# Down projection of three quarters of the FFN by Strassen's scheme, its products between blocks of the up projection

## The chip, the cores and the metric

The kernel runs on one core of one Trainium2 chip. The metric is the device time of one execution in microseconds (us), the median over several runs. The times and rows below come from the kernel as it was before the change.

## What is computed

One post-norm layer of an encoder, batch 1, 512 tokens, width 1024. The first sublayer mixes tokens (a state-space branch and a dilated attention branch, gated, projected) and ends in a LayerNorm. The change touches the second sublayer only:

```
f = jnp.square(jax.nn.relu(h @ w_up)) @ w_down      # w_up 1024 x 4096, w_down 4096 x 1024
h = layer_norm(alpha * h + f, ln2_g, ln2_b)         # alpha = 2 ** 0.25
```

All data are float32. To keep precision each operand is split into a part rounded to the matmul's type (hi) and the remainder (lo), and a product is three matmuls: hi x hi, hi x lo, lo x hi (`mm3`, lines 134 to 136).

## The kernel before

TensorE multiplies a stationary block of 128 x 128 by up to 512 columns and adds into one of eight banks of PSUM. The 4096 inner units are 32 blocks of 128. Up gives, for one block, 128 units x 512 tokens: 8 steps over the 1024 inputs, 3 matmuls each (`up_mm`, line 914), so 24 matmuls of 512 columns. ScalarE takes the relu out of PSUM (line 960), VectorE squares it (961), ScalarE rounds it to "fh" (962), VectorE forms the remainder "fl" (963).

Down works in two halves f of 16 blocks, each after its 16 up blocks, and in two column halves c of 512 (lines 946 to 999). For a pair of unit blocks and a column half there is one weight tile of 128 x 1024 floats, 512 KB. For each, `down_mm` issues 4 token tiles x 2 blocks x 3 = 24 matmuls. When all pairs are done, VectorE adds the bank into the residual "h1" (993 in the first half, with alpha; 998 in the second, followed by LayerNorm statistics, 999). In the last half and columns the last four pairs (ND) are held back and worked tile by tile, so that the LayerNorm of one token tile (941 to 943, 1001 to 1006) runs under the matmuls of the next.

Weights come through one stream, `ws` (class `Stream`, lines 73 to 126): SyncE's queue (SP) loads a raw tile (three buffers, line 87), ScalarE casts it to "wh" (108), VectorE subtracts to "wl" (109), two buffers each, one tile ahead of use. These two splits have raised priority. The first four up blocks (NU) have their weights split early into the pool "wu" and run in two halves of 256 tokens while the first LayerNorm ends.

The order of instructions on each engine is made by a scheduler at compile time from data dependencies, buffer slots and priorities (the order of the text, where nothing else decides). A pool opened where another was closed waits for the tiles there. GpSimd does nothing in this part of the kernel; earlier it adds and multiplies tiles for the state-space branch (lines 361, 366, 435, 485).

Of the kernel before, what the change touches and what calls it, by code (L numbers as in the profile page):

```python
# [43 lines left out]
def hybrid_layer_kernel(ctx: ExitStack, tc: tile.TileContext, t: dict, out: bass.AP):  # L44
# [817 lines left out]

    rot = [3, 4, 0, 1, 6, 7, 5, 2]
    nrot = [0]

    def next_bank(name):
        nrot[0] += 1
        return bank(rot[(nrot[0] - 1) % 8], name)
# [76 lines left out]
    st2 = [lp.tile([P, 3, 6], F32, name=f"st2_{i}") for i in range(4)]  # L945
    for f in range(2):
        ff = []
        if f == 0:
            g2 = load_ln(1)
        for i in range(16):  # L950
            if f == 0 and i < NU:
                ps = pre[i]
                up_mm(ps, *wu[i], slice(256, 512))
            else:
                ps = next_bank(f"ps_u{f}_{i}")
                up_mm(ps, *ws.get(), slice(0, 512))
            rl = fp.tile([P, S], F32, name=f"rl{f}_{i}", tag="rl", bufs=2)
            fh = fp.tile([P, S], F32R, name=f"fh{f}_{i}", tag="fh", bufs=17)
            fl = fp.tile([P, S], F32R, name=f"fl{f}_{i}", tag="fl", bufs=17)
            act.activation(rl, ps, AF.Relu)  # L960
            dve.tensor_mul(rl, rl, rl)
            act.copy(fh, rl)
            dve.tensor_sub(fl, rl, f32(fh))
            ff.append((fh, fl))
        if f == 0:
            wu_ctx.close()
            held["dn"] = ctx.enter_context(tc.tile_pool(name="dn", bufs=1, side="right", reuse_waits="tile"))
        for c in range(2):
            cs = slice(c * 512, (c + 1) * 512)
            tail = ND if (f, c) == (1, 1) else 0  # L970
            pss = [[next_bank(f"ps_d{f}_{c}_{i}_{q}") for q in range(2 if tail and i == 3 else 1)] for i in range(4)]

            def down_mm(i, kp, w, parts=(0, 1)):
                ts_ = slice(i * P, (i + 1) * P)
                n = 512 // len(pss[i])
                for q in range(len(pss[i])):
                    if q in parts:
                        for kk in range(2):
                            k = kp * 2 + kk
                            ws_ = slice(kk * 512 + q * n, kk * 512 + q * n + n)  # L980
                            mm3(pss[i][q][:, :n], [(ff[k][0][:, ts_], ff[k][1][:, ts_])], [(w[0][:, ws_], w[1][:, ws_])], first=(k == 0), last=(k == 15))

            for kp in range(8 - tail):
                w = ws.get()
                for i in range(4):
                    down_mm(i, kp, w)
            wt = [ws.get() for _ in range(tail)]
            for i in range(4):
                for part in ((0,), (1,)) if len(pss[i]) > 1 else ((0, 1),):
                    for q in range(tail):  # L990
                        down_mm(i, 8 - tail + q, wt[q], part)
                if f == 0:
                    dve.scalar_tensor_tensor(h1[i][:, cs], h1[i][:, cs], ALPHA, pss[i][0], op0=ALU.mult, op1=ALU.add)
                else:
                    n = 512 // len(pss[i])
                    for q, ps in enumerate(pss[i]):
                        hs = slice(c * 512 + q * n, c * 512 + q * n + n)
                        dve.tensor_add(h1[i][:, hs], h1[i][:, hs], ps[:, :n])
                        dve.bn_stats(st2[i][:, c + q, :], h1[i][:, hs])
                if tail:  # L1000
                    mv = lp.tile([P, 32], F32, name=f"mvb{i}", tag="bmv", bufs=2)
                    dve.bn_aggr(mv[:, 0:2], st2[i][:, :2 + i // 3, :])
# [65 lines left out]
```

## Time and profile before

| what | value |
|---|---|
| median of 3 runs | 1027.06 us (1026.61 to 1027.87) |
| the profiled execution | 1027.38 us |
| its span, first to last instruction | 1025.6 us |
| granted TensorE clock, mean | 0.999 of full |
| instructions | 13697 |
| HBM read, written | 128.25 MB, 11.30 MB |

The profile is of one execution. Its span leaves 1.8 us of the device time outside. Engines are PE (TensorE matmul), PEld (its weight load, which overlaps), DVE (VectorE), ACT (ScalarE), POOL (GpSimd) and SP (SyncE, which issues the DMAs). A group is named by line, engine, operation and tiles, output before input; "L109" is line 109. Idle time of an engine is put down to what released it. Matmuls are pipelined, so that the duration of one is longer than the step from one to the next.

### The profile page before, as it was taken

The page shows a single profiled execution, that of the slowest core. Times are in us where ns is not written, and L with a number is a line of the kernel's source. Part 1 is how long each engine was busy: PE and PEld are TensorE (multiplying, and loading weights), DVE is VectorE, ACT ScalarE, POOL GpSimd, SP SyncE. Part 2 cuts the span into 40 slices and gives each one's busy share as a digit, 9 for nine tenths or more (in the row PEclk, how much of TensorE's full clock was granted, in tenths as well). Part 3 has the DMA queues.
Part 4 walks back from the last instruction along what each step waited for, and adds up shares of the span by engine and source line. Part 5 has one row for each costly group of instructions (what it writes and reads, how often), then busy time and mean ns, then how long its engine had stood idle before and what let it go on. Part 6 is the DMA issues. An engine that isn't in the chain of part 4 may idle for free.

```text
span 1025.6 us, 13697 instructions
## 1 busy us (share of the span) xinstructions
PE 1016.2 (99%) x5169; PEld 842.0 (82%) x5169; DVE 651.5 (64%) x1035; ACT 501.5 (49%) x977; POOL 73.8 (7%) x66
## 2 busy tenths in 40 slices
PE   9999999999999999999999999999999999999997
PEld 7888888888888888888778788898888888888886
DVE  4296979689979897975985285844432333443336
ACT  4444877468857875764773353223431223333120
POOL 0000201221121022112000000000000000000000
PEclk9999999999999999999999999999999999999999
DMA  6445355425653564464853278112233333333322
GB/s 237 149 150 144 113 196 166 147 78 173 179 153 111 167 203 140 150 214 154 288 155 104 62 250 289 46 42 75 90 103 101 86 100 103 94 92 103 101 84 82
DMA packets 48449, 140.42 MB, mean 137 GB/s; under 512 B 6528, under 2 KB 7424, under 8 KB 48128
## 3 DMA queue, kind: packets, MB, share of 16 engines
q1 hardware_dynamic: 48240, 139.30, 43.4%
q8 instruction: 40, 0.66, 0.3%
q10 hardware_dynamic: 144, 0.26, 0.1%
q14 instruction: 25, 0.20, 0.1%
HBM read 128.25 MB, written 11.30 MB: 136 GB/s over the span
## 4 chain that ended last, share of the span: by engine, by line
PE 90%; DVE 5%; ACT 2%; DMA 2%; issue 1%; POOL 0%; DVEq 0%; ACTq 0%; POOLq 0%
PE ps_u L135 6%; PE ps_u L136 6%; PE ps_d L136 6%; PE ps_u L134 6%; PE ps_d L134 6%; PE ps_d L135 6%; PE ps_pa L134 3%; PE ps_z L134 3%; PE ps_z L136 3%; PE ps_z L135 3%; PE ps_pa L135 3%; PE ps_pa L136 3%; PE ps_x L134 3%; PE ps_x L136 2%; PE ps_x L135 2%; PE ps_yo L481 2%
## 5 line engine op out<-in xcount | busy, mean ns | idle before, releaser
L109 DVE TENSOR_TENSOR wl<-wraw,wh 128x1024 fp32r<-128x1024 f32 (+1 forms) x165 | 201.4, 1224 | 234.7 <-ACT wh L108 230.2
L108 ACT CAST wh<-wraw 128x1024 fp32r<-128x1024 f32 (+1 forms) x165 | 171.3, 1042 | 260.8 <-PE ps_d L136 108.6
L135 PE MATMUL ps_u<-htl,wh 128*128 128x512 f32 (+1 forms) x288 | 105.3, 366 | 0.3 <-DVE htl L909 0.3
L134 PE MATMUL ps_u<-hth,wh 128*128 128x512 f32 (+1 forms) x288 | 105.3, 366 | 0.0
L136 PE MATMUL ps_u<-hth,wl 128*128 128x512 f32 (+1 forms) x288 | 105.2, 365 | 0.0
L135 PE MATMUL ps_d<-wl,fh 128*128 128x512 f32 (+1 forms) x272 | 102.5, 377 | 0.0
L134 PE MATMUL ps_d<-wh,fh 128*128 128x512 f32 (+1 forms) x272 | 102.4, 377 | 0.0
L136 PE MATMUL ps_d<-wh,fl 128*128 128x512 f32 (+1 forms) x272 | 102.4, 377 | 0.0
L135 PEld LDWEIGHTS ps_u<-htl,wh 128*128 128x128 f32 x288 | 54.3, 189 | 9.2 <-DVE htl L909 0.5
L136 PEld LDWEIGHTS ps_u<-hth,wl 128*128 128x128 f32 x288 | 54.3, 189 | 8.8
L134 PEld LDWEIGHTS ps_u<-hth,wh 128*128 128x128 f32 x288 | 54.2, 189 | 8.9 <-ACT hth L908 0.3
L135 PEld LDWEIGHTS ps_d<-wl,fh 128*128 128x128 f32 x272 | 51.2, 188 | 9.5
L134 PEld LDWEIGHTS ps_d<-wh,fh 128*128 128x128 f32 x272 | 51.2, 188 | 9.4
L136 PEld LDWEIGHTS ps_d<-wh,fl 128*128 128x128 f32 x272 | 51.2, 188 | 9.4
L134 PE MATMUL ps_pa<-yh,wh 128*128 128x512 f32 x128 | 52.1, 407 | 0.0
L450 DVE SCALAR_TENSOR_TENSOR U<-bc,acr,U 128x128 f32<-128x128 f32 x128 | 46.6, 398 | 8.6 <-ACT U L448 8.5
L134 PE MATMUL ps_g<-xh,wh 128*128 128x512 f32 x128 | 51.5, 402 | 0.0
L134 PE MATMUL ps_z<-xh,wh 128*128 128x512 f32 x128 | 50.9, 398 | 0.0
L134 PE MATMUL ps_x<-xh,wh 128*128 128x512 f32 x128 | 50.9, 398 | 0.0
L136 PE MATMUL ps_g<-xh,wl 128*128 128x512 f32 x128 | 50.0, 391 | 0.4 <-DVE wl L109 0.4
L135 PE MATMUL ps_pa<-yl,wh 128*128 128x512 f32 x128 | 50.1, 392 | 0.2 <-DVE yl L561 0.2
L136 PE MATMUL ps_pa<-yh,wl 128*128 128x512 f32 x128 | 50.1, 391 | 0.0
(262 smaller groups left out, 2185.3 us busy)
## 6 DMA issues: line engine op xcount, KB each, us to landing
wraw<-in_w_in_dram SPq DMA_DIRECT2D x68, 512.0 KB, 3.5
bc<-dr_acr SPq DMA_DIRECT2D x32, 512.0 KB, 4.4
wraw<-in_w_up_dram SPq DMA_DIRECT2D x32, 512.0 KB, 3.6
wraw<-in_w_dn_dram SPq DMA_DIRECT2D x32, 512.0 KB, 3.6
be<-dr_ear SPq DMA_DIRECT2D x32, 256.0 KB, 4.5
wraw<-in_w_ps_dram SPq DMA_DIRECT2D x16, 512.0 KB, 3.8
dr_gate<-g SPq DMA_DIRECT2D x16, 256.0 KB, 2.1
wraw<-in_w_out_dram SPq DMA_DIRECT2D x8, 512.0 KB, 4.5
```

Source lines behind the costliest of these rows:

```text
L108: act.copy(h[:, :width], r[:, :width])
L109: dve.tensor_sub(l[:, :width], r[:, :width], f32(h[:, :width]))
L134: pe.matmul(ps, lh, rh, start=(first and i == 0), stop=False)
L135: pe.matmul(ps, lh, rl, start=False, stop=False)
L136: ins = pe.matmul(ps, ll, rh, start=False, stop=(last and i == n - 1))
L450: dve.scalar_tensor_tensor(U[:, ch(c)], bcs[0][:, hh, ch(c)], acr[:, c, h:h + 1], U[:, ch(c)], op0=ALU.subtract, op1=ALU.min)
L481: pe.matmul(po[d][:, ch(c)], prev[d, c][:, pr * P:(pr + 1) * P], C[:, ch(c)], start=True, stop=True)
```

## The change

The 32 unit blocks become four chunks of 8. Chunks 0 to 2 go through a Strassen scheme in Winograd's form: tokens, units and columns are each cut in two, so that activations are 2 x 2 blocks (a11 to a22, each 4 unit blocks x 256 tokens), weights 2 x 2 quarters (b11 to b22, 1 MB each), and 7 block products stand for 8. The sums of blocks are made on GpSimd in place (`prep_product`), the split into hi and lo after the sum. A product is 24 matmuls into two banks (`product`); its results go into h1 at once, on VectorE or GpSimd. Each product of chunk ch stands behind an up block of chunk ch + 1. Chunk 3 is done as before, pair by pair, with the last column half tile by tile. The activations of a chunk stay unsplit in "r" tiles; the tiles of h (hth, htl) now lie in a pool that is closed after up, and the weights that are held back and the second LayerNorm's constants are placed there. `next_bank` goes. The cut diff (in the deleted loop only the stream's part is shown; the rest of it is printed above):

```diff
-NU, ND = 4, 4
+NU = 4
+UP_ORDER = [range(8), [4, 5, 6, 7, 0, 1, 2, 3]]
+DN_ORDER = [6, 7, 4, 5]
...
     h1 = [lp.tile([P, D], F32, name=f"h1_{i}") for i in range(4)]
-    hth = lp.tile([P, KT, S], F32R, name="hth")
-    htl = lp.tile([P, KT, S], F32R, name="htl")
-    lng = []
-
-    def load_ln(i):
-        g = lp.tile([P, 2, D], F32, name=f"ln{i}", tag="ln", bufs=1)
...
-    for f in range(2):
-        for i in range(16):
-            if f or i >= NU:
-                ws.add(t["w_up"][f * 16 + i])
-        for c in range(2):
-            for i in range(8):
-                ws.add(t["w_dn"][f, c, i], hold=("dn", i) if (f, c) == (1, 1) and i >= 8 - ND else None)
+    for ch in range(4):
+        for b in UP_ORDER[ch > 0]:
+            if ch or b >= NU:
+                ws.add(t["w_up"][ch * 8 + b])
+    for c in range(2):
+        for i in DN_ORDER:
+            ws.add(t["w_dn"][1, c, i], hold=("dn", i) if c else None)
...
+    r2 = {}
+    def up_block(ch, b):
+        if b % 4 == 0:
+            r2[ch, b // 4] = fp.tile([P, 4, S], F32, name=f"r{ch}_{b // 4}", tag=f"r{b // 4}", bufs=1 + b // 4)
+        if ch == 0 and b < NU:
+            ps = pre[b]
+            up_mm(ps, *wu[b], slice(256, 512))
+        else:
+            ps = bank((0, 1)[b % 2] if ch == 0 and b < 6 else (6, 7)[b % 2], f"ps_u{ch}_{b}")
+            up_mm(ps, *ws.get(), slice(0, 512))
+        r = r2[ch, b // 4][:, b % 4, :]
+        act.activation(r, ps, AF.Relu)
+        dve.tensor_mul(r, r, r)
+    for b in range(NU):
+        up_block(0, b)
+    wu_ctx.close()
+    wq_ctx = ExitStack()
+    qp = wq_ctx.enter_context(tc.tile_pool(name="qp", bufs=1, side="right", reuse_waits="tile"))
+    quarter = {}
+    def load_quarters(ch):
+        for half, c in ((0, 0), (0, 1), (1, 1), (1, 0)):
+            q = qp.tile([P, 2, 1024], F32, name=f"wq{ch}_{half}{c}", tag="wq", bufs=4)
+            for j in range(2):
+                dma.dma_start(q[:, j, :], t["w_dn"][ch // 2, c, (ch % 2) * 4 + half * 2 + j])
+            quarter[ch, half, c] = q
+    def prep_product(ch, p):
+        b11, b12, b22, b21 = [quarter[ch, *x] for x in ((0, 0), (0, 1), (1, 1), (1, 0))]
+        lo, hi = slice(0, 256), slice(256, 512)
+        a11, a21 = r2[ch, 0][:, :, lo], r2[ch, 0][:, :, hi]
+        a12, a22 = r2[ch, 1][:, :, lo], r2[ch, 1][:, :, hi]
+        a, asum = {1: (a11, None), 5: (a21, (a21, a22, ALU.add)), 6: (a21, (a21, a11, ALU.subtract)), 7: (a11, (a22, a21, ALU.subtract)),
+                   3: (a21, (a12, a21, ALU.subtract)), 2: (a12, None), 4: (a22, None)}[p]
+        w, wsum = {1: (b11, None), 5: (b11, (b12, b11)), 6: (b11, (b22, b11)), 7: (b12, (b22, b12)),
+                   3: (b22, None), 2: (b21, None), 4: (b21, (b21, b11))}[p]
+        if asum:
+            pool.tensor_tensor(a, asum[0], asum[1], op=asum[2])
+        ah = fp.tile([P, 4, 256], F32R, name=f"ah{ch}{p}", tag="ah", bufs=2)
+        al = fp.tile([P, 4, 256], F32R, name=f"al{ch}{p}", tag="al", bufs=2)
+        act.copy(ah, a)
+        dve.tensor_sub(al, a, f32(ah))
+        wc = []
+        for j in range(2):
+            if wsum:
+                pool.tensor_sub(w[:, j, :], wsum[0][:, j, :], wsum[1][:, j, :])
+            h = qp.tile([P, 1024], F32R, name=f"ch{ch}{p}{j}", tag="ch", bufs=2)
+            l = qp.tile([P, 1024], F32R, name=f"cl{ch}{p}{j}", tag="cl", bufs=2)
+            act.copy(h, w[:, j, :])
+            dve.tensor_sub(l, w[:, j, :], f32(h))
+            wc.append((h, l))
+        return ah, al, wc
+    BANKS = [(0, 1), (3, 4), (5, 2)]
+    npr = [0]
+    def product(ch, p, ops):
+        ah, al, wc = ops
+        pss = [bank(n, f"ps_p{ch}{p}_{n}") for n in BANKS[npr[0] % 3]]
+        npr[0] += 1
+        for j in range(2):
+            for q in range(2):
+                ts_ = slice(q * P, (q + 1) * P)
+                for kk in range(2):
+                    ws_ = slice(kk * 512, kk * 512 + 512)
+                    k = 2 * j + kk
+                    mm3(pss[q], [(ah[:, k, ts_], al[:, k, ts_])], [(wc[j][0][:, ws_], wc[j][1][:, ws_])], first=(k == 0), last=(k == 3))
+        def add(rows, c, q, term, scaled=False, eng=dve):
+            h = h1[rows * 2 + q][:, c * 512:(c + 1) * 512]
+            if scaled and ch == 0:
+                dve.scalar_tensor_tensor(h, h, ALPHA, term, op0=ALU.mult, op1=ALU.add)
+            else:
+                eng.tensor_add(h, h, term)
+        for q, ps in enumerate(pss):
+            if p == 1:
+                v[q] = fp.tile([P, S], F32, name=f"v{ch}_{q}", tag="v", bufs=2)
+                act.copy(v[q], ps)
+                add(0, 0, q, v[q], True, pool)
+            elif p == 5:
+                add(1, 1, q, ps, True)
+                add(0, 1, q, ps, True)
+            elif p == 6:
+                dve.tensor_add(v[q], v[q], ps)
+                add(0, 1, q, v[q], eng=pool)
+            elif p == 7:
+                dve.tensor_add(v[q], v[q], ps)
+                add(1, 0, q, v[q], True, pool)
+                add(1, 1, q, v[q], eng=pool)
+            else:
+                add(*{3: (0, 1), 2: (0, 0), 4: (1, 0)}[p], q, ps)
+    v = {}
+    load_quarters(0)
+    for b in range(NU, 8):
+        up_block(0, b)
+    ops = prep_product(0, 1)
+    for ch in range(3):
+        seq = [1, 5, 6, 7, 3, 2, 4]
+        for n, p in enumerate(seq):
+            up_block(ch + 1, UP_ORDER[1][n])
+            product(ch, p, ops)
+            if n < 6:
+                ops = prep_product(ch, seq[n + 1])
+        if ch < 2:
+            load_quarters(ch + 1)
+        up_block(ch + 1, UP_ORDER[1][7])
+        if ch < 2:
+            ops = prep_product(ch + 1, 1)
+    wq_ctx.close()
+    ht_ctx.close()
+    dn = held["dn"] = ctx.enter_context(tc.tile_pool(name="dn", bufs=1, side="right", reuse_waits="tile"))
+    g2 = load_ln(dn, 1)
+    ff = {}
+    def split_pair(n):
+        i = DN_ORDER[n] - 4
+        src = r2[3, i // 2][:, (i % 2) * 2:(i % 2) * 2 + 2, :]
+        if n % 2:
+            fh = fp.tile([P, 2, S], F32R, name=f"fh{n}", tag="ah", bufs=2)
+            fl = fp.tile([P, 2, S], F32R, name=f"fl{n}", tag="al", bufs=2)
+        else:
+            hl = fp.tile([P, 4, S], F32R, name=f"fhl{n}", tag="r1", bufs=2)
+            fh, fl = hl[:, 0:2, :], hl[:, 2:4, :]
+        act.copy(fh, src)
+        dve.tensor_sub(fl, src, f32(fh))
+        ff[n] = (fh, fl)
...
+    def down_mm(ps, i, n, w, q, width):
+        ts_ = slice(i * P, (i + 1) * P)
+        for kk in range(2):
+            ws_ = slice(kk * 512 + q * width, kk * 512 + (q + 1) * width)
+            mm3(ps[:, :width], [(ff[n][0][:, kk, ts_], ff[n][1][:, kk, ts_])], [(w[0][:, ws_], w[1][:, ws_])], first=(n == 0 and kk == 0), last=(n == 3 and kk == 1))
+
+    def add_out(ps, i, col, width, slot):
+        hs = slice(col, col + width)
+        dve.tensor_add(h1[i][:, hs], h1[i][:, hs], ps[:, :width])
+        dve.bn_stats(st2[i][:, slot, :], h1[i][:, hs])
+
+    for n in range(4):
+        split_pair(n)
+    pss = [bank(n, f"ps_d0_{n}") for n in (3, 4, 5, 2)]
+    for n in range(4):
+        w = ws.get()
+        for i in range(4):
+            down_mm(pss[i], i, n, w, 0, 512)
+    wt = [ws.get() for _ in range(4)]
+    for i in range(4):
+        add_out(pss[i], i, 0, 512, 0)
+    for i in range(4):
+        parts = 2 if i == 3 else 1
+        for q in range(parts):
+            ps = bank((0, 1, 6, 7, 3)[i + q], f"ps_d1_{i}{q}")
+            for n in range(4):
+                down_mm(ps, i, n, wt[n], q, 512 // parts)
+            add_out(ps, i, 512 + q * 256, 512 // parts, 1 + q)
...
```

## Rows read from the trace of the kernel before

**Rows 1.** The page of the profiled execution: span, busy time, chain that ended last.
```profile
span 1025.6 us, 13697 instructions
...
PE 1016.2 (99%) x5169; PEld 842.0 (82%) x5169; DVE 651.5 (64%) x1035; ACT 501.5 (49%) x977; POOL 73.8 (7%) x66
...
PE 90%; DVE 5%; ACT 2%; DMA 2%; issue 1%; POOL 0%; DVEq 0%; ACTq 0%; POOLq 0%
```

**Rows 2.** Busy time by stretch: us from:to, length, busy of each engine, clock, DMA share, GB/s.
```profile
691.40:1018.60 327.20, 327.20 (x1490) 272.81 (x1488) 132.50 (x159) 94.26 (x119) 0.00 (x0) 1.00 0.31 93
```

**Rows 3.** VectorE in order of time: start, length, line, operation (up, then down).
```profile
719.74 1.23 DVE L109 TENSOR_TENSOR wl<-wraw,wh 128x1024 fp32r<-128x1024 f32 x1 [2.24 <-ACT wh L108]
725.17 1.23 DVE L109 TENSOR_TENSOR wl<-wraw,wh 128x1024 fp32r<-128x1024 f32 x1 [2.23 <-ACT wh L108]
...
779.76 1.23 DVE L109 TENSOR_TENSOR wl<-wraw,wh 128x1024 fp32r<-128x1024 f32 x1 [4.21 <-ACT wh L108]
785.20 1.23 DVE L109 TENSOR_TENSOR wl<-wraw,wh 128x1024 fp32r<-128x1024 f32 x1 [4.21 <-ACT wh L108]
```

**Rows 4.** Waits from 690 us on: total us, times, longest.
```profile
ACT wh L108 <- PE ps_d L136: 108.6, 26, 4.5
```

**Rows 5.** Groups by line from 600 us on: busy us, mean ns, idle before.
```profile
L109 DVE TENSOR_TENSOR wl<-wraw,wh 128x1024 fp32r<-128x1024 f32 x72 | 87.8, 1225 | 172.7 <-ACT wh L108 172.6
...
L108 ACT CAST wh<-wraw 128x1024 fp32r<-128x1024 f32 x71 | 74.3, 1053 | 186.5 <-PE ps_d L136 108.6 <-PE ps_u L135 53.9 <-DMA wraw<-in_w_up_dram 9.7
...
L963 DVE TENSOR_TENSOR fl<-rl,fh 128x512 fp32r<-128x512 f32 x32 | 22.2, 693 | 22.0 <-ACT fh L962 22.0
...
L993 DVE SCALAR_TENSOR_TENSOR h<-h,ps_d 128x512 f32<-128x512 f32 x8 | 5.3, 685 | 2.5 <-PE ps_d L136 2.5
```

**Rows 6.** Busy time by stretch, where the loads are densest.
```profile
600.00:625.00 25.00, 25.00 (x112) 20.70 (x111) 21.17 (x29) 10.43 (x13) 0.00 (x0) 1.00 0.88 303
```

**Rows 7.** GpSimd's operations by line: ns min/median/max, first and last start.
```profile
L361 POOL TENSOR_TENSOR yt<-yt,be x16: 1268/1291/1847, 151.9 to 474.9; 128x512 f32<-128x512 f32 x16
L435 POOL TENSOR_TENSOR pv<-pv,etot x16: 1045/1055/1960, 102.1 to 414.0; 128x512 f32<-128x512 f32 x16
L485 POOL TENSOR_TENSOR be<-be x16: 732/779/1377, 126.1 to 464.6; 128x256 f32<-128x256 f32 x16
```

**Rows 8.** GpSimd and VectorE in order of time, where they overlap.
```profile
214.95 1.22 DVE L109 TENSOR_TENSOR wl<-wraw,wh 128x1024 fp32r<-128x1024 f32 x1
...
215.11 1.96 POOL L435 TENSOR_TENSOR pv<-pv,etot 128x512 f32<-128x512 f32 x1 [2.53 <-DVE pv L436]
...
216.08 0.74 DVE L284 SCALAR_TENSOR_TENSOR acc<-ps_B,vec,acc 128x510 f32<-128x510 f32 x1
...
109.04 1.05 POOL L435 TENSOR_TENSOR pv<-pv,etot 128x512 f32<-128x512 f32 x1 [2.01 <-DVE pv L436]
...
109.07 1.56 DVE L418 TENSOR_TENSOR xwl<-xw,xwh 128x512 fp32r<-128x512 f32 x1
...
171.92 1.52 POOL L366 TENSOR_TENSOR sq<-sq,sq 128x512 f32<-128x512 f32 x1 [1.47 <-ACT sq L364]
...
172.22 1.77 DVE L286 SCALAR_TENSOR_TENSOR x<-x,acc 128x512 f32<-128x512 f32 x1
```

**Rows 9.** VectorE in order of time at two places of the last down half.
```profile
971.30 1.28 DVE L998 TENSOR_TENSOR h<-h,ps_d 128x512 f32<-128x512 f32 x2
972.50 1.28 DVE L999 BATCH_NORM_STATS2 st<-h 128x6 f32<-128x512 f32 x2
...
1003.81 0.75 DVE L941 SCALAR_TENSOR_TENSOR h<-h,mvb,ln 128x512 f32<-128x512 f32 x1
1004.48 0.16 DVE L1004 RECIPROCAL mvb<-mvb 128x1 f32<-128x1 f32 x1
1004.55 0.73 DVE L941 SCALAR_TENSOR_TENSOR h<-h,mvb,ln 128x512 f32<-128x512 f32 x1
```

**Rows 10.** Busy time by stretch after the last matmul.
```profile
1018.60:1021.00 2.40, 0.10 (x1) 0.00 (x0) 2.15 (x6) 0.29 (x1) 0.00 (x0) 1.00 0.19 73
1021.00:1025.60 4.60, 0.00 (x0) 0.00 (x0) 1.73 (x3) 0.00 (x0) 0.00 (x0) 0.75 0.29 114
```

More of the change, by code (lines that the diff above doesn't have):

```diff
@@ L830, in hybrid_layer_kernel, with load_ln @@
     h1 = [lp.tile([P, D], F32, name=f"h1_{i}") for i in range(4)]
-    hth = lp.tile([P, KT, S], F32R, name="hth")
-    htl = lp.tile([P, KT, S], F32R, name="htl")
-    lng = []
-    def load_ln(i):
-        g = lp.tile([P, 2, D], F32, name=f"ln{i}", tag="ln", bufs=1)
+    st2 = [lp.tile([P, 3, 6], F32, name=f"st2_{i}") for i in range(4)]
+    ht_ctx = ExitStack()
+    hp = ht_ctx.enter_context(tc.tile_pool(name="hp", bufs=1, side="right", reuse_waits="tile"))
+    hth = hp.tile([P, KT, S], F32R, name="hth")
+    htl = hp.tile([P, KT, S], F32R, name="htl")
+    def load_ln(pool_, i):
+        g = pool_.tile([P, 2, D], F32, name=f"ln{i}")
         dma.dma_start(g, t["ln"][2 * i:2 * i + 2].rearrange("(o a) d -> o a d", o=1).to_broadcast([P, 2, D]))
@@ L861, in bank @@
         return pw.tile([P, 512], F32, name=name, tag=f"b{n}", bufs=1)
[L863 to L868, printed above, removed]
     pso_b = [(6, 7), (5, 2), (3, 4), (0, 1)]
@@ L888, in hybrid_layer_kernel @@
         if k == 0:
-            g1 = load_ln(0)
+            g1 = load_ln(held["wu"], 0)
         dma.dma_start(h1[k], t["x"][k * P:(k + 1) * P, :])
@@ L943, in ln_half @@
         dma.dma_start(out[i * P:(i + 1) * P, cs], h1[i][:, cs])
[L945 to L1002, printed above, removed]
-                    act.activation(mv[:, 1:2], mv[:, 1:2], AF.Sqrt, bias=epsv[:, 1:2])
-                    dve.reciprocal(mv[:, 1:2], mv[:, 1:2])
-                    ln_half(i, 0, mv)
-                    ln_half(i, 1, mv)
@@ new lines, in hybrid_layer_kernel @@
+    for n in range(4):
[15 more added lines that the diff above has]
+            add_out(ps, i, 512 + q * 256, 512 // parts, 1 + q)
+        mv = lp.tile([P, 32], F32, name=f"mvb{i}", tag="bmv", bufs=2)
+        dve.bn_aggr(mv[:, 0:2], st2[i][:, :1 + parts, :])
+        act.activation(mv[:, 1:2], mv[:, 1:2], AF.Sqrt, bias=epsv[:, 1:2])
+        dve.reciprocal(mv[:, 1:2], mv[:, 1:2])
+        ln_half(i, 0, mv)
+        ln_half(i, 1, mv)
```

## The prediction

> **What bounds the kernel now.** First the page's busy time: TensorE is busy 1016.2 us of a span of 1025.6 us, VectorE 64%, ScalarE 49%, GpSimd 7% [rows 1]. A busy TensorE is not yet a TensorE at its peak, so next the chain that ended last: 90% of it is TensorE, 5% VectorE [rows 1]. Then the stage that the change touches, from the first full-width up matmul at 691.4 us to the last down matmul at 1018.6 us: TensorE is busy in all of its 327.2 us at granted clock 1.00 (the 2.4 GHz level), VectorE in 132.5, ScalarE in 94.3, GpSimd in none [rows 2]. The pace inside it is read from the weight splits: in down the VectorE split of each weight tile comes 5.44 us after the one before, in up it is the same to 0.01 us [rows 3], and between two splits stand 24 matmuls of 512 columns, so 5.44 / 24 = 0.227 us each. The waits of this stage (ScalarE on "ps_d", 108.6 us) are helpers waiting for TensorE to free a buffer [rows 4]; nothing holds TensorE up. So a matmul less is 0.227 us less, as long as the other engines keep up.
>
> **What is removed.** Before, the down projection of 24 of the 32 unit blocks takes 24 blocks x 4 token tiles x 2 column halves x 3 split terms = 576 matmuls. After, it is 3 chunks x 7 products x 24 = 504. The 72 that go are 72 x 0.227 = **16.3 us**. Up (32 blocks x 24) and the last chunk's 192 down matmuls stay. A product is as dense as before: 24 matmuls of 512 columns, two banks, so 5.44 us. The weight bytes are the same 32 issues of 512 KB.
>
> **What is added on VectorE and ScalarE.** A product needs one cast on ScalarE and one subtraction on VectorE for its activations (1024 wide) and two of each for its weights: 3 x 1.05 us and 3 x 1.225 us [rows 5]. For 21 products that is 77.2 us of VectorE; it takes the place of 24 weight splits and 24 activation splits of 0.69 us, 46 us [rows 5]. The products' sums into h1 are 14 VectorE operations a chunk at 0.685 us [rows 5], some 29 us against 11 before. VectorE rises by about 50 us to some 180 of 311; ScalarE has 63 casts, 66 us, for 24 of weights, 25 us, and 24 short ones, so it rises by less than 41 us to 135. Neither is a bound by its own sum, and the stage's slack covers both. The last chunk and the tail keep their form: after the last matmul the same VectorE chain runs to the end (1018.6 to 1025.6). Quarter loads are 4 MB a chunk in 82 us, 50 GB/s on top of 93 [rows 2]; the trace has held 303 GB/s [rows 6], and chunk 0's are issued five blocks ahead of its first product. On SP's queue a quarter load that waits for its slot holds up the next up weights, of which three raw tiles lie ahead: I take nothing for it, and up to 2 us if that cover is gone. The closing of the wu, quarter and h pools in front of the new ones costs nothing as long as the block between (5.44 us) covers it. The last chunk's down weights wait for the h pool, but only those of column half 1, 20 us later; the same cover hides the four splits of pairs.
>
> **What is added on GpSimd** is the dear part. A chunk has 4 activation sums and 8 half-weight sums, 1024 wide each, and 8 adds of 512 (4 in chunk 0, where scaled adds go to VectorE). A 512 add took 1.291 us (median, yt), one of 256 columns 0.779 [rows 7]. By that slope a sum of 1024 is 1.291 + 2 x 0.512 = **2.3 us**, an estimate; bounds are twice the 1.055 us of pv, 2.11, and twice 1.291, 2.58 [rows 7]. A chunk is 12 x 2.3 + 8 x 1.29 = 37.9 us. By itself that fits in 15 x 5.44 = 81.6 us of TensorE.
>
> But GpSimd and VectorE shut each other out. A split on VectorE starts at 214.95 and takes 1.22 us; the GpSimd multiply that starts inside it takes 1.96 instead of 1.05. The other way round GpSimd starts at 109.04 and ends at 110.09; the VectorE subtraction begun at 109.07 takes 1.56 where 512 columns take 0.69, and the one at 172.22 1.77, beside an add begun at 171.92 [rows 8]. Both are cases of two SBUF operands on VectorE; the L284 operation at 216.08, which reads PSUM, takes its usual 0.74 beside a running GpSimd [rows 8]. From 1.225 and 0.693 us [rows 5] the part that excludes is about 1.04 ns an element: 1.07 us for 1024, 0.53 for 512. The Trainium skill says the same in kind (GPSIMD Engine Reference, Key points: GpSimd shares SBUF interfaces with VectorE and contends with its two-SBUF-input instructions); the rows above add that either side waits out the whole of the other.
>
> So there is a ledger of one shared port. Per chunk VectorE holds it 8 x (1.07 + 0.53) for up and 7 x 3 x 1.07 for products = 35.2 us; with GpSimd 73.1 of 81.6. It fits on average, but not where the sums crowd, in products 1, 5, 6 and 7. The stretch runs from the end of the chunk's last up block (block 3, which the first activation sum needs) to the start of product 7: U, P1, U, P5, U, P6, U, 7 x 5.44 = 38.1 us. Less the relu and square in front (1.3) and the cast and split behind (2.3), 34.5 are left. Into it must go 3 activation sums, 6 weight sums of which one is done before, and two adds: 8 x 2.3 + 2.6 = 21.0 us, and VectorE's 4 x 1.6 + 10 x 1.07 = 17.1. That is 38.1, **3.6 us short**, in chunks 1 and 2. In chunk 0 the quarters come in during blocks 4 to 7, three or four weight sums are done early, and it is short by nothing or 0.5. 2 x 3.6 + 0.5, about **8 us** of TensorE stall. With 2.11 us a sum it is 5, with 2.58 and a VectorE operation queued behind a running sum twice a chunk 14.
>
> GPSIMD Engine Reference in the Trainium skill (Performance versus the Vector engine) speaks against putting sums here at all: a two-input elementwise add is about twice as dear as on VectorE (4497 ns for 2048). Our rows agree, 1.29 against 0.69. By its figure a 1024 sum is about 2.25 us, an estimate, and the sum below would come out 1 us lower.
>
> **Sum.** The profiled execution took 1027.4 us, 0.3 above the median of the runs shown (1027.06). 1027.4 - 16.3 + 8 = 1019.1; against the median 1018.8. I say **1019**, between 1013.5 and 1025 for this case.
>
> **Rivals.**
> (a) The port is no limit: sums are made so far ahead that the stretch absorbs them. For it: buffers of the quarters allow product 7's weight sums to run early, average use of the port is only 90%. Against: the 3.6 us shortfall already counts what is made ahead. 1027.4 - 16.3 = 1011.1, up to 1013.5.
> (b) All eaten: shortfalls at the upper bound and a few late loads, 14 to 18.5 us: 1025 to 1029, no change.
> (c) Slower: GpSimd's queue order. If the adds of a product stand ahead of the next product's sums on GpSimd, then after product 6 come VectorE's add 0.69, two adds 2.6, an activation sum 2.3, a weight sum 2.3, cast and split 2.3, 10.1 us against the one up block of 5.44 that covers it: 4.7 us of stall at each such place. There are eight (behind product 1 in chunks 1 and 2, behind 6 and 7 in all three). From four of them on the gain is gone; five make 1011.1 + 23.5 = 1034.6. Against: the queues are not in the order of the text. On VectorE two adds (L998) run ahead of the first statistics (L999), and L941 ahead of L1004, as they became ready [rows 9]. For: that order was fixed without knowing the port.
> (d) The clock falls. It read 0.75 between 1021 and 1025.6, after TensorE's last matmul, so part of it was at 1.2 GHz, while in the stage it stayed 1.00 without a gap [rows 2, 10]. A stall of 4 us in front of a product could do so; a block at 1.2 GHz costs 5.44 more. Three such on top of the forecast: 1035. The Trainium skill (TensorE: Matmul & The Clock Gate, The HAM clock gate) says that idling brings TensorE to 1.2 GHz; no stall in this stage shows whether such short ones do.
> (e) The change not doing what it says would be matmuls not falling by 72; the count is fixed by the loops, so I give it nothing.
>
> **How the numbers follow.** Forecast 0.52, (a) 0.22, (b) 0.07, (c) 0.13, (d) 0.06. The measurement of this kernel can tell about 0.2%, 2 us. Faster: 0.52 + 0.22 = 0.74; same 0.07; slower 0.13 + 0.06 = 0.19. The range takes in the forecast, (a) and (b), from 1010.5 to 1029, and leaves 0.19 above.
>
> **What would show it.** Right: 72 matmuls fewer, GpSimd busy over 110 us with its 1024 sums above 2.3 us on the mean, VectorE subtractions of 1024 stretched above 1.225, TensorE idle 5 to 14 us in waits on VectorE's weight or activation remainders ahead of products 5, 6 and 7, more in chunks 1 and 2 than in 0. Wrong: sums near 1.5 us (then (a)); adds ahead of sums on GpSimd with stalls behind products 6 and 7 (c); granted clock below 1.00 in the stage (d); waits on DMA or on freed pools, which I took as nothing.

## Result and profile after

The changed kernel took **1029.92 us** (median of 15 runs, 1028.64 to 1032.14), the kernel before 1027.82 in the runs beside it (15 runs, 1026.61 to 1029.31): a ratio of 1.0023 [1.0015, 1.0031], slower by 2.1 us. The forecast was 1019 with a range up to 1029. The profiled execution took 1030.3 us with a span of 1028.5.

The page of the changed kernel answers to [rows 1]:

```profile
span 1028.5 us, 13622 instructions
...
PE 1008.0 (98%) x5073; PEld 831.7 (81%) x5073; DVE 772.3 (75%) x1084; ACT 528.1 (51%) x994; POOL 213.3 (21%) x122
...
PE 87%; DVE 7%; ACT 3%; DMA 2%; issue 1%; POOL 0%; DVEq 0%; ACTq 0%; POOLq 0%
```

TensorE is 8.2 us less busy, not 16.3, and in the chain that ended last VectorE has 7% for 5% and ScalarE 3% for 2%. GpSimd went from 73.8 to 213.3 us. From the start of the first full-width up matmul to the start of the last down matmul, called the stage from here on, the kernel before took 327.0 us and this one 329.2 (691.83 to 1021.02). A stage's time is always that of the profiled execution.

Where it went is seen in the stage cut into stretches, which answers to [rows 2] (us from:to, length, busy of TensorE, its weight load, VectorE, ScalarE and GpSimd, clock, DMA share, GB/s):

```profile
691.80:725.00 33.20, 33.20 (x149) 27.48 (x148) 24.53 (x15) 14.13 (x18) 18.72 (x7) 1.00 0.39 124
725.00:750.00 25.00, 21.54 (x88) 17.34 (x87) 22.98 (x17) 9.28 (x11) 11.26 (x4) 0.93 0.11 30
750.00:800.00 50.00, 50.00 (x222) 41.40 (x221) 35.94 (x33) 18.68 (x21) 16.23 (x8) 1.00 0.39 135
800.00:825.00 25.00, 21.35 (x83) 16.78 (x82) 21.27 (x10) 10.65 (x13) 21.79 (x9) 0.86 0.14 43
825.00:875.00 50.00, 50.00 (x222) 41.41 (x221) 43.48 (x36) 20.72 (x23) 22.23 (x11) 1.00 0.36 116
875.00:900.00 25.00, 21.36 (x91) 17.05 (x90) 15.36 (x12) 8.53 (x10) 13.62 (x5) 0.95 0.27 85
900.00:925.00 25.00, 25.00 (x103) 20.43 (x102) 23.62 (x15) 10.59 (x13) 19.96 (x7) 0.91 0.14 42
925.00:1000.00 75.00, 75.00 (x333) 62.10 (x332) 52.75 (x50) 29.25 (x31) 16.28 (x8) 1.00 0.26 78
```

One stretch in each chunk is short of TensorE by some 3.5 us (21.54, 21.35 and 21.36 of 25), and in the same stretch or the next the clock reads below 1.00. In between TensorE is as full as before. TensorE's waits in the stage name the releasers (us in total, times, longest):

```profile
PE ps_p L136 <- ACT ah L981: 3.9, 2, 1.9
PE ps_p L137 <- DVE cl L990: 3.5, 1, 3.5
PE ps_p L138 <- DVE al L982: 3.4, 2, 1.7
```

The two waits on `ah` and the two on `al` are product 1 of chunks 1 and 2, the one on `cl` is the second half of product 5 of chunk 0. Product 1 multiplies blocks that are not summed, so no late sum can hold it up. Here is product 1 of chunk 1 in order of time (start, length, engine, line; in brackets the idle time before and what ended it):

```profile
795.00 11.43 POOL L986 TENSOR_TENSOR wq<-wq,wq 128x1024 f32<-128x1024 f32 x4 [14.55 <-DVE cl L990]
...
801.63 2.55 DVE L111 TENSOR_TENSOR wl<-wraw,wh 128x1024 fp32r<-128x1024 f32 x1 [3.13 <-ACT wh L110]
...
804.11 2.87 DVE L951 TENSOR_TENSOR r<-r 128x512 f32<-128x512 f32 x1
...
807.02 1.04 ACT L981 CAST ah<-r 128x1024 fp32r<-128x1024 f32 x1 [4.93 <-DVE r L951]
807.06 2.36 POOL L978 TENSOR_TENSOR r<-r,r 128x1024 f32<-128x1024 f32 x1 [0.63 <-DVE r L951]
808.09 3.66 DVE L982 TENSOR_TENSOR al<-r,ah 128x1024 fp32r<-128x1024 f32 x2 [1.11 <-ACT ah L981]
808.11 0.50 PE L136 MATMUL ps_p<-ch,ah 128*128 128x512 f32 x1 [1.94 <-ACT ah L981]
...
810.56 0.79 PE L138 MATMUL ps_p<-ch,al 128*128 128x512 f32 x1 [1.71 <-DVE al L982]
811.15 0.63 PE L136 MATMUL ps_p<-ch,ah 128*128 128x512 f32 x1
811.57 0.63 PE L137 MATMUL ps_p<-cl,ah 128*128 128x512 f32 x1
```

As soon as the split of product 1's weights releases them, GpSimd runs four weight sums in a row, those of products 5 and 7, which nobody needs yet. Meanwhile VectorE must split the weights of the up block behind product 1 (2.55 us in place of 1.23) and then square the chunk's last up block (2.87 in place of 0.69); ScalarE stands idle for 4.93 us until that square lets it cast for product 1. Then an activation sum of 2.36 us starts 0.04 us behind the cast, and the activation remainder that product 1 waits for stands behind it. Chunk 2 is the same, its four sums at 883.27, its stalls at 896.38 and 898.83.

Over the whole stage the groups that answer to [rows 5] show the same (busy us, mean ns, idle before): a weight split takes 1582 ns for 1225, the square 1415 for 686, and GpSimd's weight sums 2893. First the square in the kernel before, then the changed kernel:

```profile
L961 DVE TENSOR_TENSOR rl<-rl 128x512 f32<-128x512 f32 x32 | 22.0, 686 | 7.4 <-ACT rl L960 7.4
```
```profile
L986 POOL TENSOR_TENSOR wq<-wq,wq 128x1024 f32<-128x1024 f32 x24 | 69.2, 2893 | 270.5 <-DVE cl L990 263.1 <-issue 7.1
L111 DVE TENSOR_TENSOR wl<-wraw,wh 128x1024 fp32r<-128x1024 f32 x34 | 53.6, 1582 | 43.7 <-ACT wh L110 43.7
L951 DVE TENSOR_TENSOR r<-r 128x512 f32<-128x512 f32 x30 | 42.5, 1415 | 4.4 <-ACT r L950 4.4
L982 DVE TENSOR_TENSOR al<-r,ah 128x1024 fp32r<-128x1024 f32 x21 | 38.1, 1815 | 8.1 <-ACT ah L981 7.6
```

Behind the stall the matmuls start 0.43 us apart instead of 0.227 (811.15, 811.57), about half pace. Three short stretches show the clock there:

```profile
738.00:740.00 2.00, 2.00 (x6) 1.52 (x6) 2.00 (x1) 0.00 (x0) 1.81 (x1) 0.50 0.56 147
811.50:815.00 3.50, 3.50 (x10) 2.65 (x9) 3.50 (x3) 0.44 (x1) 3.17 (x1) 0.50 0.30 66
899.50:903.50 4.00, 4.00 (x11) 3.14 (x10) 4.00 (x3) 0.71 (x2) 3.32 (x2) 0.50 0.32 86
```

0.50 is the 1.2 GHz level. TensorE counts as busy at it, so the busy time hides this part of the loss.

Without any loss the stage would take 310.3 us (three kernels below measure just that), so 18.9 us were lost: 329.19 - 310.30. By chunk, from the starts of the blocks less 5.44 us for each, in us:

| | chunk 0 | chunk 1 | chunk 2 | sum |
|---|---|---|---|---|
| lost in all | 5.35 | 6.67 | 6.87 | 18.9 |
| of it TensorE waiting (each gap less one step of 0.227) | 3.61 | 3.99 | 3.98 | 11.6 |
| the rest: slow matmuls behind the waits | 1.74 | 2.68 | 2.89 | 7.3 |

The 72 matmuls less gave 327.02 - 310.30 = 16.7 us, and 18.9 were taken back: 1027.8 - 16.7 + 18.9 = 1030.0.

### The profile page after: what moved, and what is told of

It reads as the page before. It is cut to its first block, busy times and chain, and to the rows that moved or that the text cites. A ratio compares the mean times of both kernels' runs of the same rounds, so it can differ in the third digit from the quotient of the medians.

```text
span 1028.5 us, 13622 instructions
## 1 busy us (share of the span) xinstructions
PE 1008.0 (98%) x5073; PEld 831.7 (81%) x5073; DVE 772.3 (75%) x1084; ACT 528.1 (51%) x994; POOL 213.3 (21%) x122
## 4 chain that ended last, share of the span: by engine, by line
PE 87%; DVE 7%; ACT 3%; DMA 2%; issue 1%; POOL 0%; DVEq 0%; ACTq 0%; POOLq 0%
PE ps_u L137 5%; PE ps_u L136 5%; PE ps_u L138 5%; PE ps_p L138 4%; PE ps_p L137 4%; PE ps_p L136 4%; PE ps_pa L136 3%; PE ps_z L136 3%; PE ps_z L138 3%; PE ps_z L137 3%; PE ps_pa L137 3%; PE ps_pa L138 3%; PE ps_x L136 3%; PE ps_x L138 2%; PE ps_x L137 2%; PE ps_yo L483 2%
## 5 line engine op out<-in xcount | busy, mean ns | idle before, releaser
L111 DVE TENSOR_TENSOR wl<-wraw,wh 128x1024 fp32r<-128x1024 f32 (+1 forms) x141 | 184.1, 1310 | 119.4 <-ACT wh L110 114.8
L110 ACT CAST wh<-wraw 128x1024 fp32r<-128x1024 f32 (+1 forms) x141 | 145.9, 1039 | 187.1 <-PE ps_u L137 79.1
L986 POOL TENSOR_TENSOR wq<-wq,wq 128x1024 f32<-128x1024 f32 x24 | 69.2, 2893 | 270.5 <-DVE cl L990 263.1
L990 DVE TENSOR_TENSOR cl<-wq,ch 128x1024 fp32r<-128x1024 f32 x42 | 74.3, 1770 | 12.4 <-ACT ch L989 12.4
L136 PE MATMUL ps_p<-ch,ah 128*128 128x512 f32 x168 | 68.1, 405 | 3.9 <-ACT ah L981 3.9
L138 PE MATMUL ps_p<-ch,al 128*128 128x512 f32 x168 | 68.5, 408 | 3.4 <-DVE al L982 3.4
L137 PE MATMUL ps_p<-cl,ah 128*128 128x512 f32 x168 | 68.1, 405 | 3.5 <-DVE cl L990 3.5
L989 ACT CAST ch<-wq 128x1024 fp32r<-128x1024 f32 x42 | 44.1, 1051 | 41.5 <-PE ps_p L138 38.0
L951 DVE TENSOR_TENSOR r<-r 128x512 f32<-128x512 f32 x32 | 43.8, 1370 | 11.5 <-ACT r L950 11.5
L437 POOL TENSOR_TENSOR pv<-pv,etot 128x512 f32<-128x512 f32 x16 | 19.8, 1238 | 148.3 <-ACT pv L435 128.6
```

The costliest lines, as they stand in the source:

```text
L110: act.copy(h[:, :width], r[:, :width])
L111: dve.tensor_sub(l[:, :width], r[:, :width], f32(h[:, :width]))
L136: pe.matmul(ps, lh, rh, start=(first and i == 0), stop=False)
L137: pe.matmul(ps, lh, rl, start=False, stop=False)
L138: ins = pe.matmul(ps, ll, rh, start=False, stop=(last and i == n - 1))
L437: pool.tensor_mul(h3(pv), h3(prev[d, c]), bc(etot[:, c, hs]))
```

## Experiments

Times are medians, of 4 runs where no number is given. Ratios are to the kernel before, with 95% intervals; the changed kernel stands at 1.0023. The theory: GpSimd's sums shut VectorE out of the shared port. Its first rival: the sums are late, since GpSimd takes long for each. The second: the clock's fall is what costs.

**Weight sums on VectorE** (GpSimd keeps the activation sums and the adds).

```diff
-                pool.tensor_sub(w[:, j, :], wsum[0][:, j, :], wsum[1][:, j, :])
+                dve.tensor_sub(w[:, j, :], wsum[0][:, j, :], wsum[1][:, j, :])
```

> The changed kernel with its 8 weight sums a chunk moved from GpSimd to VectorE; activation sums and adds stay on GpSimd. Theory P (port: a VectorE operation with two SBUF operands waits out a whole GpSimd operation): the four weight sums in a row at each chunk's start are gone, so the square of the chunk's last up block takes about 0.7 us instead of 2.9, the stalls ahead of products (10.8 us in all) shrink to under 2 us, the granted clock stays at the upper level in the stage, and the time is 1027.8 - 16.6 = 1011 to 1013 us. Rival V (VectorE's own load is the bound; it is 75% busy in the span already): VectorE gets 24 x 1.225 = 29 us more and the stalls stay or grow, 1026 us or more.

Measured: 1017.95 us, ratio 0.9906 [0.9892, 0.9921], stage 316.65. VectorE has more work and TensorE waits less. VectorE ahead of product 1 of chunk 1, then the same engine with GpSimd at product 5 of chunk 0:

```profile
801.01 0.69 DVE L951 TENSOR_TENSOR r<-r 128x512 f32<-128x512 f32 x1
802.81 3.70 DVE L982 TENSOR_TENSOR al<-r,ah 128x1024 fp32r<-128x1024 f32 x2 [1.12 <-ACT ah L981]
```
```profile
732.27 2.68 POOL L978 TENSOR_TENSOR r<-r,r 128x1024 f32<-128x1024 f32 x1 [4.10 <-DVE al L982]
732.66 3.38 DVE L990 TENSOR_TENSOR cl<-wq,ch 128x1024 fp32r<-128x1024 f32 x1
```

The square is back at 0.69 us. The longest wait left comes from an activation sum that starts just ahead of a remainder (the pair above: TensorE waits 2.49 us for that `cl`); four others are 0.50 to 0.65 us. The time is 5 us above the bound of the expectation, so the four activation sums a chunk are not free either.

**The port alone.** As the one before, and GpSimd makes four subtractions a chunk that nobody reads, at the places of products 5 and 7. No result needs them, so that a sum that is late by its own length can't be what costs.

```diff
+                if p in (5, 7):
+                    jk = qp.tile([P, 1024], F32, name=f"jk{ch}{p}{j}", tag="jk", bufs=1)
+                    pool.tensor_sub(jk, b21[:, j, :], b22[:, j, :])
```

> The kernel of e1_wsum_dve with four extra GpSimd subtractions of 1024 a chunk, at the place of the weight sums of products 5 and 7: they read two weight quarters and write a tile that nobody reads. Theory P (port): no result is later by data, but VectorE waits them out: the operations of 1024 and 512 that overlap them stretch by up to 2.4 us, the square of the chunk's last up block takes over 2 us again, product 1 of chunks 1 and 2 stalls, and 3 to 12 us of the gain of e1 go. Rival D (lateness: products waited for the results of the sums on a slow engine, not for the port): nobody waits for these, the time is that of e1 within 1 us.

Measured: 1038.45 us, ratio 1.0117 [1.01, 1.0134]: 20.5 us more than without the idle work, though nothing depends on it. Its waits from 690 us on, GpSimd's line, and VectorE and GpSimd ahead of product 1 of chunk 1:

```profile
PE ps_p L136 <- ACT ah L981: 9.6, 2, 4.8
PE ps_p L138 <- DVE al L982: 2.4, 2, 1.2
PE ps_p L137 <- DVE cl L993: 2.4, 1, 2.4
PE ps_u L138 <- DVE wl L111: 2.4, 1, 2.4
```
```profile
L988 POOL TENSOR_TENSOR jk<-wq,wq 128x1024 f32<-128x1024 f32 x12 | 35.5, 2962 | 262.5 <-DMA wq<-in_w_dn_dram 261.8
```
```profile
799.20 3.41 DVE L993 TENSOR_TENSOR cl<-wq,ch 128x1024 fp32r<-128x1024 f32 x1
...
811.68 0.68 DVE L951 TENSOR_TENSOR r<-r 128x512 f32<-128x512 f32 x1
...
812.44 2.36 POOL L978 TENSOR_TENSOR r<-r,r 128x1024 f32<-128x1024 f32 x1 [7.56 <-DVE r L951]
```

The largest stalls are the same ones, at product 1 of chunks 1 and 2 behind the square. The square itself takes 0.68 us here, not over 2 as expected: it comes late, since VectorE's operations ahead of it were held (that `cl` 3.41 us for 1.22). GpSimd's own queue isn't late either: GpSimd has been idle for 7.56 us when its next real sum starts. Lateness falls; exclusion is shown, and dearer than expected (3 to 12 us). 12 subtractions of 2.96 us are 35.5 us of GpSimd, and the end comes 20.5 us later; part of that is the clock, whose mean went from 0.998 to 0.987.

**Activation sums on VectorE** (GpSimd keeps the weight sums and the adds), the other half.

```diff
-            pool.tensor_tensor(a, asum[0], asum[1], op=asum[2])
+            dve.tensor_tensor(a, asum[0], asum[1], op=asum[2])
```

> The changed kernel with only the 4 activation sums a chunk on VectorE; the 8 weight sums stay on GpSimd. Theory P with the burst of four weight sums at a chunk's start as the main cause: product 1 of chunks 1 and 2 still waits 3 us or more for its activations and the clock falls behind it: 1020 to 1029 us, worse than e1. Rival (the activation sums, which stand in the chain of products 5, 6, 7, are the main cause): 1011 to 1018 us, as good as e1 or better.

Measured: 1020.93 us, ratio 0.9931 [0.9916, 0.9945], stage 319.57. The 1.94-us waits on `ah` at product 1 stay, as the theory has it, since the four weight sums in a row stay; those on `al` shrink to 0.6. The stage loses 6.4 us with the activation sums alone on GpSimd (316.65 - 310.30), 9.3 with the weight sums alone, 18.9 with both. The 9.3 are rather low: this kernel's profiled execution took 1019.13 us, the shortest of its four.

**Each GpSimd sum in two halves**: the same work, but the port can change hands twice as often.

```diff
-            pool.tensor_tensor(a, asum[0], asum[1], op=asum[2])
+            for hb in (slice(0, 2), slice(2, 4)):
+                pool.tensor_tensor(a[:, hb, :], asum[0][:, hb, :], asum[1][:, hb, :], op=asum[2])
...
-                pool.tensor_sub(w[:, j, :], wsum[0][:, j, :], wsum[1][:, j, :])
+                for hs in (slice(0, 512), slice(512, 1024)):
+                    pool.tensor_sub(w[:, j, hs], wsum[0][:, j, hs], wsum[1][:, j, hs])
```

> The changed kernel with each GpSimd sum of 1024 cut into two of 512 (about 1.3 us each). GpSimd's work grows by some 0.2 us a sum. Theory P (port, each side waits out the whole of the other's current operation): a VectorE operation waits at most 1.3 us instead of 2.4 at a time, the longest drop from 3.4 to about 2.4 us, the three stalls shrink to about half (4 to 6 us in all) and the clock falls less: 1015 to 1022 us. Rival D (lateness: GpSimd's throughput): sums finish later than before, 1029 to 1034 us.

Measured: 1025.9 us (10 runs), ratio 0.9979 [0.9967, 0.9992], stage 324.99. Half the grain, some 4 us of the 18.9 back: the length of one operation counts, but most of the loss stays, and neither forecast (1015 to 1022 by the port, 1029 or more by lateness) was met. Two stretches of this kernel, behind the same pair of stalls (2.1 us on `ch` and 0.77 on `cl`) in chunk 1 and in chunk 2:

```profile
831.00:834.00 3.00, 2.23 (x6) 1.54 (x6) 3.00 (x3) 2.14 (x3) 0.00 (x0) 0.57 0.03 5
921.00:924.00 3.00, 2.23 (x9) 1.63 (x10) 3.00 (x3) 2.28 (x3) 0.00 (x0) 1.00 0.00 0
```

The clock fell behind the first and not behind the second. The same wait at the same place doesn't always cost the clock. The ten runs suggest what it costs here: they differ in their mean granted clock, and the four at 0.993 took 1026.2 to 1027.7 us, the three at 0.997 1022.2 to 1023.8, some 4 us less.

**Fillers in the waits.** To part the wait from the clock, 16 matmuls, whose results the product overwrites, go where TensorE waits at product 1 of chunks 1 and 2.

```diff
+                    if p == 1 and ch and q == 0 and k == 0:
+                        fill = lambda: [pe.matmul(pss[1], hth[:, 0, 0:P], wc[0][0][:, 0:512], start=True, stop=True) for _ in range(8)]
+                        fill()
+                        pe.matmul(pss[0], ah[:, 0, ts_], wc[0][0][:, ws_], start=True, stop=False)
+                        pe.matmul(pss[0], ah[:, 0, ts_], wc[0][1][:, ws_], start=False, stop=False)
+                        fill()
+                        pe.matmul(pss[0], al[:, 0, ts_], wc[0][0][:, ws_], start=False, stop=False)
+                        continue
```

> The changed kernel with 16 extra matmuls of 512 columns ahead of and inside the start of product 1 in chunks 1 and 2, 8 where TensorE waited 1.94 us for ah and 8 where it waited 1.71 us for al; their results are overwritten. Theory C (the stall itself is only about 3.6 us each, and TensorE going idle brings the clock to the 1.2 GHz level for the matmuls behind it): with TensorE busy through these two stalls the granted clock stays at the upper level there, the 11 and 12 matmuls that stepped 0.43 us step 0.227, and 4 to 5.5 us are saved: 1024.4 to 1026 us. Rival: the clock falls for another reason or the fillers are not hidden: no gain, up to 32 x 0.227 = 7.3 us more, 1030 to 1037 us.

Measured: 1028.0 us (10 runs), ratio 1.0007 [0.9998, 1.0017], stage 327.80. The clock stays at 1.00 there, but only 1.4 us of the stage come back, which neither side of the expectation had: new waits of 0.45 and 0.51 us on `cl` stand at products 5 and 6 of both chunks.

**Fillers in chunk 0 too**, 15 of them in a bank that nobody reads, in front of the matmul that waits for `cl` in product 5.

```diff
+                    if p == 5 and ch == 0 and q == 0 and k == 2:
+                        fb = bank(5, "fill_b")
+                        pe.matmul(pss[0], ah[:, 2, ts_], wc[1][0][:, ws_], start=False, stop=False)
+                        [pe.matmul(fb, hth[:, 0, 0:P], wc[0][0][:, 0:512], start=True, stop=True) for _ in range(15)]
+                        pe.matmul(pss[0], ah[:, 2, ts_], wc[1][1][:, ws_], start=False, stop=False)
+                        pe.matmul(pss[0], al[:, 2, ts_], wc[1][0][:, ws_], start=False, stop=False)
+                        continue
```

> As the kernel with filler matmuls at product 1 of chunks 1 and 2, and 15 more fillers in the second half of product 5 of chunk 0, where TensorE still waited 3.45 us for a weight remainder and 8 matmuls behind it took 0.43 us; their results go to a bank that nobody reads. The wait itself is only filled, not shortened. If the fall of the clock costs by itself, the granted clock is 1.00 in the whole stage and 8 x 0.20 = 1.6 us go: a stage of 326.2 for 327.8, about 1026.4 us, ratio 0.9991. If the port's debt sets the time and a slow TensorE only lets it be paid off unseen, the 1.6 us come back as new waits for VectorE behind product 5 of chunk 0, and the time stays at 1028.0, ratio 1.0007.

Measured: 1026.96 us (11 runs), ratio 0.9996 [0.9987, 1.0005], stage 326.26. The stretches of 25 us around the three places (columns as above), and all TensorE waits of the stage:

```profile
725.00:750.00 25.00, 24.90 (x111) 20.28 (x110) 24.35 (x19) 9.57 (x11) 11.47 (x4) 1.00 0.14 44
800.00:825.00 25.00, 24.38 (x105) 19.29 (x105) 23.64 (x10) 10.93 (x14) 21.79 (x9) 1.00 0.14 42
900.00:925.00 25.00, 24.02 (x104) 19.00 (x103) 25.00 (x14) 10.84 (x13) 18.19 (x7) 1.00 0.14 43
```
```profile
PE ps_p L137 <- DVE cl L990: 1.9, 4, 0.5
PE ps_p L1011 <- ACT ah L981: 0.3, 2, 0.2
```

The stage is the 326.2 of the first theory, and no wait is new behind product 5 of chunk 0; the ratio's interval holds the first theory's 0.9991 and not the rival's 1.0007. So in these traces the clock costs by itself in chunk 0 (the intervals of the two filler kernels overlap, so their times alone don't show it). In chunks 1 and 2 the rival is mostly right: of the 2.4 to 2.6 us saved at product 1, 1.8 come back at products 5 and 6. With the clock at 1.00 throughout, the stage still loses 16.0 us, by chunk 3.8, 6.1 and 6.1. Up to 0.8 of it is the fillers' own, which run past the waits by 0.2 to 0.3 us a place (4.29 against 3.99 at product 1). So between these two executions **the port takes 15.2 to 16.0 us, the clock 2.9 to 3.7**. The ratios, 1.0023 and 0.9996, differ by 2.8 us, give or take 1.2.

**All sums and adds on VectorE.** GpSimd idles in the stage.

```diff
-            pool.tensor_tensor(a, asum[0], asum[1], op=asum[2])
+            dve.tensor_tensor(a, asum[0], asum[1], op=asum[2])
...
-                pool.tensor_sub(w[:, j, :], wsum[0][:, j, :], wsum[1][:, j, :])
+                dve.tensor_sub(w[:, j, :], wsum[0][:, j, :], wsum[1][:, j, :])
...
-                add(0, 0, q, v[q], True, pool)
+                add(0, 0, q, v[q], True)
```

(and the other three adds with `pool` likewise)

> The changed kernel with all sums and all adds on VectorE; GpSimd does nothing in this stage. Theory P (port): no VectorE operation is stretched, all of 1024 take 1.22 us and all of 512 0.69; VectorE has some 71 us of work in 81.6 us of TensorE a chunk; stalls under 2 us in all, clock at the upper level, 1011 to 1013.5 us, better than e1 (1018). Rival V (VectorE is full): nothing is stretched, but VectorE runs without a gap through products 1 to 7 and TensorE waits for it, 1015 to 1024 us.

Measured: **1010.34 us**, ratio 0.983 [0.9814, 0.9847], better than both kernels. Its stage and its sums and remainders on VectorE:

```profile
691.40:990.00 298.60, 298.60 (x1319) 247.22 (x1318) 226.85 (x248) 122.18 (x137) 0.00 (x0) 1.00 0.29 92
```
```profile
L990 DVE TENSOR_TENSOR cl<-wq,ch 128x1024 fp32r<-128x1024 f32 x42 | 51.2, 1222 | 16.2 <-ACT ch L989 16.2
...
L986 DVE TENSOR_TENSOR wq<-wq,wq 128x1024 f32<-128x1024 f32 x24 | 28.9, 1220 | 0.1
L982 DVE TENSOR_TENSOR al<-r,ah 128x1024 fp32r<-128x1024 f32 x21 | 25.6, 1220 | 2.2 <-ACT ah L981 2.2
```

TensorE waits nowhere. VectorE does 36 sums and 20 adds more than in the changed kernel and is busy for less: 236.4 us of the whole stage, against 255.4 there, where its operations wait for the port. At 1.22 us each, as its subtractions in [rows 5], they wait for nothing here.

**Only the sums on VectorE**, the adds left on GpSimd (both sum lines of the diff above).

> The changed kernel with all 12 sums a chunk on VectorE; only the adds of 512 columns into h1 stay on GpSimd. Theory P: a VectorE operation waits at most 1.3 us, behind products 1, 6 and 7 only: 1011 to 1015 us, near e5 and better than e1. Rival V: VectorE full, as e5, 1015 us or more, but less than e5, since the adds are off it.

Measured: 1010.81 us, ratio 0.9836 [0.9822, 0.9851], stage 310.30, no waits. The 20 adds of 512 on GpSimd (33.7 us), by themselves, cost nothing that can be told: it is the sums of 1024 that matter.

**No sums at all**, the floor of this scheme (its products multiply blocks that are not summed, so it doesn't compute the layer):

```diff
-        if asum:
-            pool.tensor_tensor(a, asum[0], asum[1], op=asum[2])
...
-            if wsum:
-                pool.tensor_sub(w[:, j, :], wsum[0][:, j, :], wsum[1][:, j, :])
```

> The changed kernel without the 12 sums a chunk (products then multiply unsummed blocks); splits, products and adds are all there. It prices all that the sums cost. The 72 fewer matmuls alone would give 1027.3 - 16.6 = 1010.7 us. Theory P: 1010.5 to 1012.5 us, no stall over 0.5 us. If the gain of the matmuls itself falls short (products denser in waits, pools, loads, splits), it stays above 1013 us.

Measured: 1010.47 us, ratio 0.9833 [0.9818, 0.9847], stage 310.30 to the hundredth as in the two kernels before. So the sums on VectorE cost no time: TensorE covers them whole.

## Why the prediction was wrong

**The removed matmuls: right.** 16.3 us were forecast; the stage without stalls is 327.02 - 310.30 = 16.7 us shorter, the medians 17 to 18 (1028.0 against 1010.3 to 1010.8).

**VectorE and ScalarE: right that neither is a bound.** VectorE without the sums, "some 180 of 311", is 198.7 of 310.6 in the kernel without sums, some 19 us more; with all sums it is 236.4 and still holds nothing up. ScalarE has 122.6 where at most 135 was said. DMA, SP's queue and the closed pools, taken at nothing, appear in no wait of TensorE. (The quarter loads' 50 GB/s are not "on top of 93": the weight bytes are the same, so the 93 has them already.)

**GpSimd's sums: right by themselves.** 2.3 us was the estimate; the one at 807.06, with no VectorE operation ahead of it in the port, took 2.36. The 2.25 us estimated from the Trainium skill (GPSIMD Engine Reference, Performance versus the Vector engine) was 0.11 short, and its rule that VectorE does such work in about half the time holds in the trace: 1.22. The rule spoke against the change's choice of engine, and the forecast let it move the sum by 1 us only.

**The shared port: the right mechanism, mis-sized; this is the step that failed.** The ledger gave "3.6 us short, in chunks 1 and 2", "0.5" in chunk 0, about 8 us, at most 14. With the clock held up it is 6.1, 6.1 and 3.8, 15 to 16 in all, and that alone eats nearly all of the 16.7 us gained. It failed in two ways, both by adding up a stretch as if the port went to whatever is due first.
First, it goes to what comes first, a whole operation at a time. A sum running, or four in a row, holds off a 0.69-us square that a product waits for; so the stall stood at product 1, where the ledger had nothing, and not "ahead of products 5, 6 and 7". The sums "made ahead" were counted there as a relief; they did the harm. The kernel with idle work, which stalls at product 1 again, bears this out, and so does the half-grain kernel: at a mean clock of 0.997 it takes 1022.2 to 1023.8 us, about 4 less than the kernel with the clock held up.
Second, chunk 0 was taken as nearly free because its quarters are early. Its stall came from an activation sum, product 6's, which can't be early, since it overwrites a block that product 5's own remainder still reads (the wait on `al` in its row); at 732.70 it started 0.38 us ahead of the weight remainder that TensorE needed. The sum ends at 735.37 and the remainder 1.08 us later, at 736.45; 1.07 is what the ledger booked for one, so it waited out the whole sum.

```profile
732.70 2.67 POOL L978 TENSOR_TENSOR r<-r,r 128x1024 f32<-128x1024 f32 x1 [1.23 <-DVE al L982]
...
733.08 3.37 DVE L990 TENSOR_TENSOR cl<-wq,ch 128x1024 fp32r<-128x1024 f32 x1
...
736.50 0.50 PE L137 MATMUL ps_p<-cl,ah 128*128 128x512 f32 x1 [3.46 <-DVE cl L990]
```

The time that TensorE visibly waited, 11.6 us, lies inside the forecast's 5 to 14, but that agreement is partly luck: the slow matmuls behind each stall hide some waits that would have come later.

**Rival (d), the clock: happened, priced wrong, given too little.** It came at all three places. Read from the matmuls it is 7.3 us, taken away it is 2.9 to 3.7; the forecast's 5.44 a place was a whole block, and 8 to 12 of a block's 24 matmuls were slow. The Trainium skill (TensorE: Matmul & The Clock Gate, The HAM clock gate) has idling lower the clock, and the trace agrees: 0.50 behind stalls of 3.46 us and of 1.94 with 1.71. The forecast asked for "a stall of 4 us"; its own ledger put 3.6 us into each of chunks 1 and 2, near that, and it should have carried the clock in the main case and not at 0.06 beside it.

**The other rivals.** (a), the port no limit, falls by the kernel with idle work. (c), adds ahead of sums, does stand in GpSimd's queue (in chunk 1 an add of product 1 at 817.88, a weight sum at 820.12), but its stalls of 4.7 us don't: TensorE waits nowhere behind products 6 and 7, and behind product 1 of chunks 1 and 2 it waits only in the kernels with fillers, at most 0.5 us. (b), all eaten, is the nearest, at 1025 to 1029, with the port's price inside its "14 to 18.5 us" (by its own sum 1011.1 + 18.5 is 1029.6), and the clock on top of it puts the time 0.9 us above 1029. It had a chance of 0.07.

**The order of the chances.** The bounds of the stall, 5 and 14, came from the bounds of one sum (2.11 to 2.58) and, above, two queued VectorE operations a chunk; the order on the port was in neither. A port booked at 73.1 of 81.6 us by the ledger's own average, with single operations of 2.4 us against 8.5 of slack a chunk, was no ground to hold 0.74 for faster.

What stays open: why in the half-grain kernel the clock fell behind one of two like stalls; what a fall costs in general, since the fillers got back some 3 of the 7.3 us while the half-grain kernel's runs differ by 4 with the clock; and how the 6.1 us of chunks 1 and 2 split between order and amount; no run put GpSimd's sums in another order.

## What to carry to other kernels

Before giving elementwise work to an idle GpSimd, ask whether VectorE has room: here it had room for all 36 sums, at half the price each and with no wait, and the same change then gained 1.7%. If both must work at once, add up their whole operations as one queue, look for the shortest operation on the path to TensorE and charge it the longest run of the other engine's operations that can start ahead of it. And where a forecast has TensorE wait several us at a time, put matmuls at half pace behind the wait into the same sum.

## What the hardware showed unasked

- An operation with two SBUF operands on VectorE waits out the whole GpSimd operation that is ahead of it: 0.69 us became 2.87, 1.21 became 3.37 to 3.42, and GpSimd's 2.36 became up to 3.38. Idle work on GpSimd cost 20.5 us, the clock's share included, more than half of its own 35.5.
- A slower TensorE can partly pay for itself: in the changed kernel, behind the fall of the clock in chunks 1 and 2 there were no waits at products 5 and 6; with the clock held up there were four of 0.47 to 0.51 us. A wait of 2.49 us (weight sums on VectorE) left the clock at 1.00, and one of 1.94 and 0.59 with two matmuls between (activation sums on VectorE) brought it down.
- Moving work onto the busier engine made that engine less busy, 236.4 us for 255.4, since the page counts waiting for the port as busy.
